# Moving a 64 KB prior ahead of the first load in a mixture-of-softmaxes kernel

## The chip, the cores and the metric

The kernel runs on one core of a Trainium2 chip. The metric is the device time of one execution in microseconds (us); lower is better. A run on one core is compared with runs of the kernel before on the same chip in the same rounds. "MB" is 10^6 bytes.

## The reference

```python
# logits: 32 x 128 x 4 x 4096 float32, prior: 32 x 128 x 4 float32
prior_probs = softmax(prior, axis=-1)            # over the 4 heads
softmax     = softmax(logits, axis=-1)           # over 4096 entries, for each head
mixture     = np.sum(prior_probs[..., None] * softmax, axis=2)   # 32 x 128 x 4096
```

268.4 MB of logits come in, 67.1 MB of result go out, and the prior is 64 KB.

## The kernel before

The rows are worked in 32 units of 128 rows. A unit's load is 8.4 MB (128 partitions of 64 KB), its store 2.1 MB. ScalarE (ACT) takes the exponentials with their sums, VectorE (DVE) the reciprocals and the weighted sum of the four heads, GpSimd (POOL) the small products of coefficients. Loads go out on SP's queue into two buffers, stores on ACT's queue (the last few on SP's). Unit 0 is loaded in two halves, and the first half has already been pulled ahead of the barrier with which the program opens:

```python
def early_first_load(nc):
    blocks = nc.main_func.blocks
    first = next((b, i) for b in blocks[1:] for i in b.instructions
                 if i.engine == mybir.EngineType.SP and i.opcode == "DMACopy")
    block, ins = first
    ...
    block.instructions.remove(ins)
    at = next(...)                     # SP's Drain in the opening block
    blocks[0].instructions.insert(at, ins)
...
        load(0)                                   # SP: two halves, 4.2 MB each
        nc.scalar.dma_start(out=pr, in_=pv)       # ACT: the prior, 16 rows of 4 KB
        load(1)                                   # SP: 8.4 MB
        nc.gpsimd.memset(pn, 0.0)
        nc.vector.reduce_max(pmax, pr, axis=AX.X)
        ...                                       # softmax of the prior, transposes into pp
            if u + 2 < U:
                load(u + 2)                       # waits for unit u's first add
```

The prior's weights `pp` are first read when unit 0's coefficients are formed.

The softmax here doesn't subtract the row's maximum and nothing guards it: scores larger than these inputs give would overflow.

Of the kernel before, what the change touches and what calls it, by code (L numbers as in the profile page):

```python
# [10 lines left out]
AX = mybir.AxisListType  # L11


def early_first_load(nc):





    blocks = nc.main_func.blocks  # L20
    first = next(
        (b, i)
        for b in blocks[1:]
        for i in b.instructions
        if i.engine == mybir.EngineType.SP and i.opcode == "DMACopy"
    )
    block, ins = first
    assert not ins.sync_info.on_wait
    block.instructions.remove(ins)
    at = next(  # L30
        n
        for n, i in enumerate(blocks[0].instructions)
        if i.engine == mybir.EngineType.SP and i.opcode == "Drain"
    )
    blocks[0].instructions.insert(at, ins)


@with_exitstack
def kernel(
    ctx: ExitStack,  # L40
    tc: tile.TileContext,
    logits: bass.AP,
    prior: bass.AP,
    out: bass.AP,
):
    nc = tc.nc
    nc.at_finalize(early_first_load)
    B, S, H, V = logits.shape
    assert prior.shape == (B, S, H)
    assert out.shape == (B, S, V)  # L50
    P = 128
    J = 2
    R = P * J
    G = B * S // R
    U = G * J
    assert G * R == B * S and G <= 32 and H == 4

    lg = logits.rearrange("b s h v -> (b s) h v").rearrange("(g p j) h v -> g j p h v", p=P, j=J)
    ov = out.rearrange("b s v -> (b s) v").rearrange("(g p j) v -> g j p v", p=P, j=J)
    pv = prior.rearrange("b s h -> (b s) h").rearrange("(g r) h -> g r h", r=R)  # L60

    cpool = ctx.enter_context(tc.tile_pool(name="cpool", bufs=1))
    psum = ctx.enter_context(tc.tile_pool(name="psum", bufs=1, space=bass.MemoryType.PSUM))



    before = {}

    def only(ins, *keep):
        for k in keep:  # L70
            tc.add_manual_dep(
                ins.ins,
                k.ins.name,
                mybir.DependencyInfo(mybir.DependencyClass.Sync, mybir.DependencyReason.DATA),
                reason="all that this instruction waits for",
            )
        tc.declare_no_dep(
            ins.ins,
            group="loop",
            keep=[k.ins for k in keep] + before.get(ins.ins.engine, []),  # L80
            reason="covered by the waits that are kept",
        )
        tc.add_to_no_dep_group("loop", ins.ins)
        before[ins.ins.engine] = [ins.ins]
        return ins


    ltile = cpool.tile([P, 2, H, V], FP32, name="ltile")
    loads = {}
    exps = {}  # L90
    adds = {}
    stores = {}

    def load(u):
        if u == 0 or u >= U - 3:
            cuts = (0, 2, 3, 4) if u == U - 1 else (0, 2, 4)
        else:
            cuts = (0, H)
        for h, to in zip(cuts, cuts[1:]):
            ld = nc.sync.dma_start(  # L100
                out=ltile[:, u % 2, h:to], in_=lg[u // J, u % J, :, h:to, :]
            )


            if u >= 2:
                only(ld, adds[u - 2, 0] if h == 0 else exps[u - 2, to - 1])
            else:
                only(ld)
            for k in range(h, to):
                loads[u, k] = ld  # L110

    def store(u, acc, eng, lo=0, hi=V):
        st = eng.dma_start(out=ov[u // J, u % J, :, lo:hi], in_=acc[:, lo:hi])
        stores[u] = only(st, adds[u, H - 1])


    pr = cpool.tile([G, R, H], FP32, name="pr")
    pn = cpool.tile([32, H, R], FP32, name="pn")
    pmax = cpool.tile([G, R], FP32, name="pmax")
    pp = cpool.tile([P, J, H, 32], FP32, name="pp")  # L120


    dsum = cpool.tile([P, U, H], FP32, name="dsum")
    rden = cpool.tile([P, U, H], FP32, name="rden")
    coeff = cpool.tile([P, U, H], FP32, name="coeff")



    ebuf1 = cpool.tile([P, V], FP32, name="ebuf1")
    ebuf2 = psum.tile([P, V], FP32, name="ebuf2")  # L130
    ebuf3 = cpool.tile([P, V], FP32, name="ebuf3")
    obuf = cpool.tile([P, 2, V], FP32, name="obuf")

    with tc.manual_schedule():
        load(0)
        nc.scalar.dma_start(out=pr, in_=pv)
        load(1)
        nc.gpsimd.memset(pn, 0.0)  # L138
        nc.vector.reduce_max(pmax, pr, axis=AX.X)  # L139
        nc.vector.tensor_sub(pr, pr, pmax.unsqueeze(2).to_broadcast([G, R, H]))  # L140
        nc.scalar.activation(pr, pr, AF.Exp)  # L141
        nc.vector.reduce_sum(pmax, pr, axis=AX.X)  # L142
        nc.vector.reciprocal(pmax, pmax)  # L143
        nc.vector.tensor_mul(  # L144
            pn[0:G].rearrange("g h r -> g r h"), pr, pmax.unsqueeze(2).to_broadcast([G, R, H])
        )
        pq = pn.rearrange("g h (p j) -> g j h p", j=J)
        for t in range(P // 32):
            nc.vector.transpose(pp[32 * t : 32 * (t + 1)], pq[:, :, :, 32 * t : 32 * (t + 1)])  # L149

        for u in range(U):
            bufd = u < U - 2
            lt = ltile[:, u % 2]
            acc = obuf[:, u % 2] if bufd else lt[:, 0]
            es = (lt[:, 0], ebuf1, ebuf2, ebuf3) if bufd else [lt[:, h] for h in range(H)]
            ppu = pp[:, u % J, :, u // J]

            def exp(h, *keep):
                ex = nc.scalar.activation(  # L159
                    es[h], lt[:, h], AF.Exp, accum_out=dsum[:, u, h : h + 1]  # L160
                )
                keep = (loads[u, h],) + keep
                if bufd and h and u:
                    keep += (adds[u - 1, h],)
                exps[u, h] = only(ex, *keep)

            def weigh(h, n, *keep):
                rc = nc.vector.reciprocal(rden[:, u, h : h + n], dsum[:, u, h : h + n])  # L168
                only(rc, exps[u, h + n - 1])
                mul = nc.gpsimd.tensor_mul(  # L170
                    coeff[:, u, h : h + n], rden[:, u, h : h + n], ppu[:, h : h + n]
                )
                return only(mul, rc, *keep)

            def add(h, mul, lo=0, hi=V):
                if h == 0:
                    st = nc.vector.tensor_scalar(  # L177
                        out=acc[:, lo:hi], in0=es[h][:, lo:hi], scalar1=coeff[:, u, h : h + 1],
                        scalar2=None, op0=ALU.mult,
                    )  # L180
                    adds[u, h] = only(st, mul)
                else:
                    st = nc.vector.scalar_tensor_tensor(  # L183
                        out=acc[:, lo:hi], in0=es[h][:, lo:hi], scalar=coeff[:, u, h : h + 1],
                        in1=acc[:, lo:hi], op0=ALU.mult, op1=ALU.add,
                    )
                    adds[u, h] = only(st, mul, adds[u, h - 1])

            free = (stores[u - 2],) if bufd and u >= 2 else ()

            m = H if u < U - 4 else 2
            for h in range(H):
                late = h == H - 1 and 4 <= u < U - 3
                if h == H - 1 and 0 < u < U - 3:
                    store(u - 1, obuf[:, (u - 1) % 2], nc.scalar)
                exp(h, *((stores[u - 4],) if late else ()))
                if (h + 1) % m:
                    continue
                g = h + 1 - m
                mul = weigh(g, m, *(free if g == 0 else ()))  # L200
                for k in range(g, h + 1):
                    n = 2 if u == U - 1 and k == H - 1 else 1
                    w = V // n
                    for c in range(n):
                        add(k, mul, c * w, (c + 1) * w)
                        if n > 1:
                            store(u, acc, nc.sync, c * w, (c + 1) * w)
            if u + 2 < U:
                load(u + 2)
            if u == U - 3:  # L210
                store(u - 1, obuf[:, (u - 1) % 2], nc.sync)
                store(u, acc, nc.sync)
            elif u == U - 2:
                store(u, acc, nc.sync)
# [30 lines left out]
```

## Time and profile before

| | before |
|---|---|
| device time, median of 6 runs | 781.04 us (780.79 to 781.23) |
| span from first to last instruction | 779.28 us |
| bytes moved | 335.66 MB, mean 431 GB/s |
| DVE, ACT busy | 67%, 60% |

The span is taken from the first instruction, which is SP's issue of unit 0's first half at 0.00. The time of a profiled run is 1.78 to 1.80 us longer than its span (the one of before took 781.07), in every run but one, which is named below. Two more lines matter later, the DMA queues on the page of before (packets, MB, share of the 16 engines' span; q1 is SP's queue, q10 is ACT's):

```profile
q1 hardware_dynamic: 6048, 276.83, 82.3%
q10 hardware_dynamic: 4064, 58.79, 17.6%
```

Nearly all of q10 is stores; the prior is 0.07 MB of it.

### The profile page before, as it was taken

The page shows a single profiled execution, that of the slowest core. Times are in us where ns is not written, and L with a number is a line of the kernel's source. Part 1 is how long each engine was busy: PE and PEld are TensorE (multiplying, and loading weights), DVE is VectorE, ACT ScalarE, POOL GpSimd, SP SyncE. Part 2 cuts the span into 40 slices and gives each one's busy share as a digit, 9 for nine tenths or more (in the row PEclk, how much of TensorE's full clock was granted, in tenths as well). Part 3 has the DMA queues.
Part 4 walks back from the last instruction along what each step waited for, and adds up shares of the span by engine and source line. Part 5 has one row for each costly group of instructions (what it writes and reads, how often), then busy time and mean ns, then how long its engine had stood idle before and what let it go on. Part 6 is the DMA issues. An engine that isn't in the chain of part 4 may idle for free.

```text
span 779.3 us, 654 instructions
## 1 busy us (share of the span) xinstructions
DVE 521.0 (67%) x174; ACT 466.7 (60%) x258; POOL 8.3 (1%) x41
## 2 busy tenths in 40 slices
DVE  4447875558755587555775557855578655689886
ACT  4476555775457755577555675546765567657782
POOL 0000000000000000000000000000000000000000
DMA  9999999999999999999999999999999999999998
GB/s 407 457 417 401 470 407 434 428 461 428 405 467 403 458 420 433 442 443 418 431 454 407 454 408 467 420 415 447 432 442 417 463 399 463 410 427 433 434 429 377
DMA packets 10117, 335.66 MB, mean 431 GB/s; under 512 B 1136, under 2 KB 1136, under 8 KB 1152
## 3 DMA queue, kind: packets, MB, share of 16 engines
q1 hardware_dynamic: 6048, 276.83, 82.3%
q10 hardware_dynamic: 4064, 58.79, 17.6%
q14 instruction: 5, 0.04, 0.0%
HBM read 268.50 MB, written 67.11 MB: 431 GB/s over the span
## 4 chain that ended last, share of the span: by engine, by line
DMA 64%; ACT 27%; DVE 6%; issue 2%; POOL 0%; DVEq 0%; POOLq 0%
DMA ltile<-in_logits_dram 62%; ACT ebuf L159 19%; ACT ltile L159 8%; DVE obuf L177 5%; DMA out_dram<-obuf 2%; DVE ltile L183 1%; POOL coeff L170 0%; DVE rden L168 0%; DVEq L240 0%; POOLq L240 0%; POOLq L170 0%
## 5 line engine op out<-in xcount | busy, mean ns | idle before, releaser
L183 DVE SCALAR_TENSOR_TENSOR obuf<-ebuf,coeff,obuf 128x4096 f32<-128x4096 f32 x90 | 403.6, 4484 | 3.8 <-POOL coeff L170 0.6
L159 ACT ACTIVATE ebuf<-ltile 128x4096 f32<-128x4096 f32 x90 | 322.9, 3589 | 7.4 <-DMA ltile<-in_logits_dram 7.4
L159 ACT ACTIVATE ltile<-ltile 128x4096 f32<-128x4096 f32 x38 | 137.3, 3614 | 280.6 <-DMA ltile<-in_logits_dram 280.6
L168 DVE RECIPROCAL rden<-dsum 128x4 f32<-128x4 f32 (+1 forms) x36 | 6.3, 175 | 227.9 <-ACT ebuf L159 225.1
L177 DVE TENSOR_SCALAR obuf<-ltile,coeff 128x4096 f32<-128x4096 f32 x30 | 70.6, 2353 | 10.2 <-POOL coeff L170 10.2
L183 DVE SCALAR_TENSOR_TENSOR ltile<-ltile,coeff 128x4096 f32<-128x4096 f32 (+1 forms) x7 | 27.0, 3875 | 0.8 <-POOL coeff L170 0.6
L159 ACT ACTIVATION_READ_ACCUMULATOR ebuf<-ltile 128x1 f32 x90 | 16.8, 186 | 0.0
L170 POOL TENSOR_TENSOR coeff<-rden,pp 128x4 f32<-128x4 f32 (+1 forms) x36 | 7.2, 200 | 755.3 <-DVE rden L168 745.4
L159 ACT ACTIVATION_READ_ACCUMULATOR ltile<-ltile 128x1 f32 x38 | 7.1, 186 | 0.0
L139 DVE TENSOR_REDUCE pmax<-pr 16x256 f32<-16x1024 f32 x1 | 1.2, 1208 | 7.8 <-DMA pr<-in_prior_dram 7.8
L141 ACT ACTIVATE pr<-pr 16x1024 f32<-16x1024 f32 x1 | 1.1, 1055 | 7.8 <-DVE pr L140 7.8
L177 DVE TENSOR_SCALAR ltile<-ltile,coeff 128x4096 f32<-128x4096 f32 x2 | 4.7, 2354 | 0.6 <-POOL coeff L170 0.6
L144 DVE TENSOR_TENSOR pn<-pr,pmax 16x1024 f32<-16x1024 f32 x1 | 1.9, 1939 | 0.1
L141 ACT ACT_TABLE_LOAD x1 | 1.3, 1283 | 1.2 <-PEq L229 1.2
L142 DVE TENSOR_REDUCE pmax<-pr 16x256 f32<-16x1024 f32 x1 | 1.2, 1207 | 1.1 <-ACT pr L141 1.1
L149 DVE STREAM_TRANSPOSE pp<-pn 32x256 f32<-32x256 f32 x4 | 1.7, 435 | 0.1
L143 DVE RECIPROCAL pmax<-pmax 16x256 f32<-16x256 f32 x1 | 1.7, 1741 | 0.0
L140 DVE TENSOR_TENSOR pr<-pr,pmax 16x1024 f32<-16x1024 f32 x1 | 1.2, 1211 | 0.0
L138 POOL MEMSET pn<- 32x1024 f32 x1 | 0.9, 941 | 0.3 <-POOLq L229 0.3
L229 POOL MEMSET const-bfloat16-1.0<- 128x1 bf16 x1 | 0.1, 106 | 0.0
L229 POOL MEMSET const-uint8-127<- 128x1 uint8 x1 | 0.1, 106 | 0.0
L229 POOL MEMSET const-float32-0.0<- 128x1 f32 x1 | 0.1, 103 | 0.2 <-issue 0.2
(1 smaller groups left out, 0.1 us busy)
## 6 DMA issues: line engine op xcount, KB each, us to landing
out_dram<-obuf ACTq DMA_DIRECT2D x28, 2048.0 KB, 29.4
ltile<-in_logits_dram SPq DMA_DIRECT2D x7, 4096.0 KB, 26.1
ltile<-in_logits_dram SPq DMA_DIRECT2D x2, 2048.0 KB, 30.9
out_dram<-obuf SPq DMA_DIRECT2D x2, 2048.0 KB, 33.9
out_dram<-ltile SPq DMA_DIRECT2D x1, 2048.0 KB, 17.2
out_dram<-ltile SPq DMA_DIRECT2D x2, 1024.0 KB, 4.8
ltile<-in_logits_dram SPq DMA_DIRECT2D x28, 30.9
pr<-in_prior_dram ACTq DMA_DIRECT2D x1, 64.0 KB, 7.0
```

Source lines behind the costliest of these rows:

```text
L139: nc.vector.reduce_max(pmax, pr, axis=AX.X)
L140: nc.vector.tensor_sub(pr, pr, pmax.unsqueeze(2).to_broadcast([G, R, H]))
L141: nc.scalar.activation(pr, pr, AF.Exp)
L142: nc.vector.reduce_sum(pmax, pr, axis=AX.X)
L143: nc.vector.reciprocal(pmax, pmax)
L144: nc.vector.tensor_mul(pn[0:G].rearrange("g h r -> g r h"), pr, pmax.unsqueeze(2).to_broadcast([G, R, H]))
L149: nc.vector.transpose(pp[32 * t : 32 * (t + 1)], pq[:, :, :, 32 * t : 32 * (t + 1)])
L159: ex = nc.scalar.activation(es[h], lt[:, h], AF.Exp, accum_out=dsum[:, u, h : h + 1])
L168: rc = nc.vector.reciprocal(rden[:, u, h : h + n], dsum[:, u, h : h + n])
L170: mul = nc.gpsimd.tensor_mul(coeff[:, u, h : h + n], rden[:, u, h : h + n], ppu[:, h : h + n])
L177: st = nc.vector.tensor_scalar(out=acc[:, lo:hi], in0=es[h][:, lo:hi], scalar1=coeff[:, u, h : h + 1], scalar2=None, op0=ALU.mult,)
L183: st = nc.vector.scalar_tensor_tensor(out=acc[:, lo:hi], in0=es[h][:, lo:hi], scalar=coeff[:, u, h : h + 1], in1=acc[:, lo:hi], op0=ALU.mu ...
```

## The change

The intent: have the prior come first, so that its softmax no longer waits behind large load packets, and take the issue off ACT. The prior goes to the head of SP's queue, and both it and the first half of unit 0 are issued ahead of the opening barrier.

```diff
-def early_first_load(nc):
+def early_transfers(nc):
...
+    body = next(b for b in blocks[1:] if of_sp(b, "DMACopy"))
+    for ins in of_sp(body, "DMACopy")[:2]:
+        assert not ins.sync_info.on_wait
+        body.instructions.remove(ins)
+        drain = of_sp(blocks[0], "Drain")[0]
+        blocks[0].instructions.insert(blocks[0].instructions.index(drain), ins)
...
     with tc.manual_schedule():
+        nc.sync.dma_start(out=pr, in_=pv)
         load(0)
-        nc.scalar.dma_start(out=pr, in_=pv)
         load(1)
```

More of the change, by code (lines that the diff above doesn't have):

```diff
@@ L11, with of_sp @@
 AX = mybir.AxisListType
-def early_first_load(nc):
+def early_transfers(nc):
     blocks = nc.main_func.blocks
-    first = next(
-        (b, i)
-        for b in blocks[1:]
-        for i in b.instructions
-        if i.engine == mybir.EngineType.SP and i.opcode == "DMACopy"
-    )
-    block, ins = first
-    assert not ins.sync_info.on_wait
-    block.instructions.remove(ins)
-    at = next(
-        n
-        for n, i in enumerate(blocks[0].instructions)
-        if i.engine == mybir.EngineType.SP and i.opcode == "Drain"
-    )
-    blocks[0].instructions.insert(at, ins)
+    def of_sp(block, opcode):
+        return [
+            i
+            for i in block.instructions
+            if i.engine == mybir.EngineType.SP and i.opcode == opcode
+        ]
+    body = next(b for b in blocks[1:] if of_sp(b, "DMACopy"))
[4 more added lines that the diff above has]
+        blocks[0].instructions.insert(blocks[0].instructions.index(drain), ins)
 @with_exitstack
@@ L46 @@
     nc = tc.nc
-    nc.at_finalize(early_first_load)
+    nc.at_finalize(early_transfers)
     B, S, H, V = logits.shape
```

## The prediction

> **What bounds the kernel now.** I read the page from the top: the busy shares first, then the slices with the DMA row, then the table of stretches, then the chain of waits, and last the opening and the first unit in the timeline.
>
> ```profile
> DVE 521.0 (67%) x174; ACT 466.7 (60%) x258; POOL 8.3 (1%) x41
> DMA  9999999999999999999999999999999999999998
> DMA packets 10117, 335.66 MB, mean 431 GB/s; under 512 B 1136, under 2 KB 1136, under 8 KB 1152
> ```
>
> No compute engine is above 67%, while the DMA engines are at nine tenths or more in 39 of 40 slices. The stretches (length, busy time of DVE, ACT and POOL, clock, DMA share, GB/s) say where the rate is not full:
>
> ```profile
> 0.00:25.00 25.00, 9.04 (x9) 12.26 (x7) 1.15 (x5) 1.00 1.02 422
> 100.00:400.00 300.00, 197.89 (x63) 176.72 (x98) 2.61 (x13) 1.00 1.00 433
> 770.00:779.30 9.30, 3.42 (x2) 0.00 (x0) 0.00 (x0) 1.00 0.76 318
> ```
>
> In the middle the transfers run at 433 GB/s. 335.66 MB at that rate are 775.2 us of the span of 779.3, so only 4.1 us in all are not explained by bytes. The start lacks 25 x (1 - 422/433) = 0.64 us and the last stretch 9.3 x (1 - 318/433) = 2.5 us; the rest is rounding and the middle's small dips. So the start can give back at most about 0.6 us, unless bytes vanish, and the change removes none. The stretch shares are coarse (a short one can show over 1), so I take only sums of long ones.
>
> The chain of waits confirms it (start us, us, what):
>
> ```profile
> 0.79 21.57 DMA ltile<-in_logits_dram
> 22.39 7.32 ACT ebuf L159 x4
> ...
> 30.22 2.37 DVE obuf L177
> 32.60 31.96 DMA ltile<-in_logits_dram
> ```
>
> The prior is not in it. The chain does pass through compute: unit 2's load is only issued at 32.60, after unit 0's first add. But in the timeline unit 1's first exp starts at 41.73, on a load that was issued at 1.18. So at 32.60 the load queue still has some 9 us of unit 1 to move, and the queue doesn't run dry. What sets the end is when the stream of load bytes begins and how fast it runs, and not when an early compute instruction ends.
>
> The opening and the prior's own path, in the timeline (start us, us, engine, line):
>
> ```profile
> 0.00 0.38 SPq L100 DMA_DIRECT2D ltile<-in_logits_dram  x1
> 0.79 0.33 SPq L100 DMA_DIRECT2D ltile<-in_logits_dram  x1
> 0.79 0.39 ACTq L136 DMA_DIRECT2D pr<-in_prior_dram  x1
> 7.81 1.21 DVE L139 TENSOR_REDUCE pmax<-pr 16x256 f32<-16x1024 f32 x1 [7.81 <-DMA pr<-in_prior_dram]
> 16.45 1.78 DVE L149 STREAM_TRANSPOSE pp<-pn 32x256 f32<-32x256 f32 x4
> 29.98 0.20 POOL L170 TENSOR_TENSOR coeff<-rden,pp 128x4 f32<-128x4 f32 x1 [28.26 <-DVE rden L168]
> ```
>
> The first half of unit 0 is already ahead of the opening barrier: issued at 0.00, with the second half and the prior both at 0.79 behind it. The prior's softmax ends at 16.45 + 1.78 = 18.23. The first reader of its result, the coefficient at 29.98, waits for the denominators. The prior has 29.98 - 18.23 = 11.75 us to spare.
>
> **What the Trainium skill says.** "Perfetto Trace Analysis", section Roofline, holds that one core streaming alone is bounded by its 16 DMA engines at about 435 GB/s; the 433 above agree. "DMA: Bandwidth & Descriptors", section Issuing engines are not separate DMA queues, says that transfers started from different engines end up on the same 16 DMA engines and interleave, so that moving an issue saves only sequencer time. The trace agrees: the prior's 64 KB took 7.0 us to land beside the first half of unit 0. The same page, Anatomy of one DMA, gives some 2 us of fixed cost for a transfer (fitted there for the GpSimd path), mostly the receipt after the last byte. Here the first half lands 12.6 us after its issue and the second at 0.79 + 21.57 = 22.36, 9.7 us later, which is just 4.19 MB at 431 GB/s. So the fixed part of a single transfer is 12.63 - 9.73 = 2.9 us, and a transfer behind another in the same queue does not pay it again: it overlaps.
>
> **The change, part by part.**
> The words of the change say that prior and first half are issued early, but the first half was early before. What is new is the prior alone.
> 1. Removed: one issue on ACT's queue (0.39 us at 0.79). ACT next loads its table at 1.21 and then has nothing to do until its exp of the prior at 10.29. Worth 0 at the end.
> 2. Added: one issue on SP, ahead of the first half. In the trace, two issues behind each other on SP start 0.39 us apart (0.79 and 1.18). So the first half is issued at about 0.39 where it was at 0.00. This is on the path: the stream of load bytes starts 0.39 us later. Cost +0.39 us.
> 3. In that gap the prior's own bytes move. 64 KB at 431 GB/s are 0.15 us; before, they took their share out of the same engines a little later. So 0.15 us of the 0.39 are not lost. Credit -0.15 us. Sum of 2 and 3: +0.24 us.
> 4. Moved: SP comes to the opening barrier about 0.39 us later, so the second half goes out at about 1.18 in place of 0.79, unit 1 at about 1.57 in place of 1.18, and POOL's memset and ACT's table load also slide by 0.4. The first half keeps the queue full until about 10 us, so none of these is waited for. Cost 0.
> 5. Gained off the path: the prior no longer shares the engines with the first half's large packets. An estimate from the fixed 2.9 us above is a landing about 2 to 3 us after issue, against 0.79 + 7.0 = 7.8. DVE's five operations on the prior and its four transposes start about 5 us earlier and end at about 13.3 in place of 18.23. Slack grows from 11.75 to about 17 us. Worth 0. ACT does its exp of the prior at about 5.4 instead of 10.29, in time where it was idle either way.
>
> So unit 0 lands at about 12.9 and 22.6, every later load slides by the same 0.24, the span is 779.5 and the time 781.04 + 0.24 = 781.3 us.
>
> **The rivals.**
> - The start is pre-paid. If the first transfer of a queue pays a start-up of its own that the prior now pays, the first half follows at once and begins no later, and what the prior saves by not sharing may even show. For it: 2.9 us of fixed cost, of which I can't see how much comes before the first byte, and a start that lacks 0.64 us of bytes. Against: SP must still spend 0.39 us on the first issue before it can make the second. It would make 780.8 to 781.0.
> - The prior's landing matters. If the early compute were on the path, 5 us less would show and the time would be about 776. Against it: 11.75 us of slack, and ACT's first exp of logits at 12.66 is released by its own load, not by the prior. I give it almost nothing.
> - The prior's fixed cost is paid in series. If the first half could not stream until the prior's receipt was in, the whole stream would start 2 to 2.9 us later: 783 to 784. Against it: the two halves land 9.7 us apart, with no gap between transfers of one queue. A few per cent.
> - The interleaving of loads and stores takes another phase. The chain goes through a store near the end (18.06 us, from 700.23, before a coefficient at 718.42), and the first periods of two units differ from the later ones (start of the load piece at 32.60, 82.00 and 129.75; later every 48.35). A shift of 0.24 us could be swallowed or doubled there. This is worth some 0.3 us either way and is most of my range.
>
> **Range and chances.** The three times of before lie within 0.19 us, so the noise is small against the terms. The centre is 781.3. Downwards the pre-paid start reaches 780.8. Upwards the full 0.39 without credit gives 781.4, and a phase shift on top of it some 781.9. A serial fixed cost lies outside. 2% are 15.6 us; nothing above comes near that, as even the whole start, with the prior on the path, is 5 us. I give 0.01 to faster, 0.98 to within 2% and 0.01 to slower.
>
> **What would show each step right or wrong.** In the timeline of the changed kernel: the prior's issue at 0.00 on SP's queue and the first half's at about 0.39 (step 2), the second half's at about 1.2 (step 4), DVE's first reduction at about 3 and not 7.81 (step 5). The first exp of logits should start at about 12.9 and the exp behind the second half at about 22.6 (sum of 2 and 3): at 12.66 and 22.39 or earlier the start was pre-paid; at 15 the fixed cost was in series. The load pieces of the chain after 300 us should stand 0.2 to 0.3 later than before, with the same 48.35 us between them. If the opening shows +0.24 and the end another amount, the phase of the stores took or added the rest. The prediction is wrong as a whole if the middle rate departs from 433 GB/s, since 1% of it is 7.8 us.

## The result, and the profile after

| | before | after |
|---|---|---|
| median of 6 runs | 781.04 us (780.79 to 781.23) | 781.41 us (781.36 to 782.33) |
| span of the profiled run | 779.28 us | 779.58 us |

The ratio is 1.0007, with a 95% interval of 0.9995 to 1.002: the same within 2%, and the interval includes 1. A ratio here is the mean time of one kernel's fast runs over that of the other's in the same rounds, so one long run (782.33) weighs on it and not on the medians. In rank the difference is clear: all six runs of after are longer than all six of before. By medians it is +0.37 us.

The page of after names the same bytes and the same busy shares. Its queue lines show the move: 32 packets (16 of data and 16 that tell of the landing) have gone from q10 to q1.

```profile
q1 hardware_dynamic: 6080, 276.89, 82.3%
q10 hardware_dynamic: 4032, 58.72, 17.6%
```

The opening in the timeline of after (start us, us, engine, line, what, idle time before):

```profile
0.00 0.39 SPq L134 DMA_DIRECT2D pr<-in_prior_dram  x1
0.45 0.42 SPq L99 DMA_DIRECT2D ltile<-in_logits_dram  x1
1.28 0.33 SPq L99 DMA_DIRECT2D ltile<-in_logits_dram  x1
2.26 1.21 DVE L138 TENSOR_REDUCE pmax<-pr 16x256 f32<-16x1024 f32 x1 [2.26 <-DMA pr<-in_prior_dram]
10.86 1.78 DVE L148 STREAM_TRANSPOSE pp<-pn 32x256 f32<-32x256 f32 x4
29.96 0.20 POOL L169 TENSOR_TENSOR coeff<-rden,pp 128x4 f32<-128x4 f32 x1 [27.75 <-DVE rden L167]
```

The prior lands 2.2 us after its issue where it took 7.0, and its weights are ready at 12.64 and not at 18.23. The coefficient that reads them still starts at 29.96 (29.98 before). The first half of unit 0 is issued 0.45 us later. Now the first exp of units 0, 1 and 2, in the timeline of before:

```profile
12.66 3.62 ACT L159 ACTIVATE ltile<-ltile 128x4096 f32<-128x4096 f32 x1 [1.31 <-DMA ltile<-in_logits_dram]
41.73 3.62 ACT L159 ACTIVATE ltile<-ltile 128x4096 f32<-128x4096 f32 x1 [12.04 <-DMA ltile<-in_logits_dram]
64.58 3.62 ACT L159 ACTIVATE ltile<-ltile 128x4096 f32<-128x4096 f32 x1 [8.35 <-DMA ltile<-in_logits_dram]
```

And in that of after:

```profile
12.64 3.62 ACT L158 ACTIVATE ltile<-ltile 128x4096 f32<-128x4096 f32 x1 [6.83 <-DMA ltile<-in_logits_dram]
41.70 3.62 ACT L158 ACTIVATE ltile<-ltile 128x4096 f32<-128x4096 f32 x1 [12.03 <-DMA ltile<-in_logits_dram]
64.97 3.62 ACT L158 ACTIVATE ltile<-ltile 128x4096 f32<-128x4096 f32 x1 [8.77 <-DMA ltile<-in_logits_dram]
```

This was the surprise. Units 0 and 1 land when they did before, in spite of the later issue; the difference appears between 42 and 65 us, while unit 2's load and the first store are under way. After that it stays. Load pieces of the chain of waits, before and then after:

```profile
82.00 30.32 DMA ltile<-in_logits_dram
...
323.93 30.91 DMA ltile<-in_logits_dram
...
662.50 30.89 DMA ltile<-in_logits_dram
```

```profile
82.39 30.32 DMA ltile<-in_logits_dram
...
324.25 30.91 DMA ltile<-in_logits_dram
...
662.80 30.89 DMA ltile<-in_logits_dram
```

**A closer look at the packets.** The trace holds a record of each DMA packet: queue, start, duration and bytes, though not which of the 16 engines moved it. Packets follow each other without a gap, and most of one size take the same time: 0.61 us for the 16 KB of a store packet, 1.21 for 32 KB of a half, 2.42 for 64 KB of a unit (medians). A few take longer. I call the excess the stretch of a packet; summed over packets and divided by 16 engines it is a time of the whole stream. (Each engine's first large packet is stretched in every kernel, 0.5 to 0.7 us in this sense; the columns below leave that out.) Sewing packets together where one starts as another ends gives what one engine does. This is worked out from the records and is not a view of the profile (an engine's chain can be swapped for that of another in step with it). The columns are start in us, queue, size, duration in us, and the stretch at the places that matter:

```
before                          after
 1.05 q1   32 KB  1.89           1.05 q1    4 KB  0.30   the prior
 2.94 q1   32 KB  1.21           1.65 q1   32 KB  1.93   first half begins
 4.14 q1   32 KB  1.21           3.58 q1   32 KB  1.21
 5.35 q10   4 KB  0.16 prior     4.78 q1   32 KB  1.21
 5.51 q1   32 KB  1.55 +0.34     5.99 q1   32 KB  1.21
 7.06 q1   32 KB  1.21           7.20 q1   32 KB  1.21
...
48.22 q1   64 KB  2.45          48.30 q1   64 KB  2.79   +0.37
50.66 q10  16 KB  0.61          51.08 q10  16 KB  0.61   first store begins
51.27 q1   64 KB  2.42          51.69 q1   64 KB  2.46
...
60.33 q1   64 KB  2.88 +0.46    60.84 q1   64 KB  2.91   +0.49   unit 2's last packet
63.21 q10  16 KB  0.61          63.75 q10  16 KB  0.61
```

Two things are read from it. First, before, the prior costs the load stream 0.16 us of its own and a stretch of 0.34 in the packet behind it. Second, after, that stretch is gone, and one of about the same size stands where the first store comes in. From 50.7 us on, load and store packets alternate with no stretch until unit 2's last packet. "DMA: Bandwidth & Descriptors", section Queues, rings and completion order, of the Trainium skill says that each engine goes round its queues packet by packet; the alternation of one q1 and one q10 packet agrees. It doesn't tell of a stretch.

The **lag** sums this up: at a time t, it is t less the transfer work done by then, where work is the usual duration of each packet, summed and divided by 16 engines. With equal bytes, the lag that is left in the steady state is what a kernel loses.

| lag in us, at | 5 us | 45 us | 66 us | 100 us | stretch 5 to 45 | stretch 45 to 66 |
|---|---|---|---|---|---|---|
| before | 1.76 | 2.12 | 2.63 | 2.56 | 0.42 | 0.56 |
| after | 2.15 | 2.09 | 3.00 | 2.93 | 0.00 | 0.96 |

At 100 us the lags differ by 2.93 - 2.56 = 0.37 us. That this is just the difference of the medians is in part luck: the spans of these two traces differ by 0.30, and the second trace of before (below) has a lag of 2.38. Read one trace to about 0.2 us. The start is 2.15 - 1.76 = 0.39 later; the prior's missing stretch gives that back by 45 us; and between 45 and 66 us it is lost again. So is the cost the start, or is it the first store? The experiments are about that.

### The profile page after: what moved, and what is told of

Its sections match the earlier page's. It is cut to its first block, busy times and chain, and to the rows that moved or that the text cites. A ratio compares the mean times of both kernels' runs of the same rounds, so it can differ in the third digit from the quotient of the medians.

```text
span 779.6 us, 654 instructions
## 1 busy us (share of the span) xinstructions
DVE 521.0 (67%) x174; ACT 466.7 (60%) x258; POOL 8.3 (1%) x41
## 4 chain that ended last, share of the span: by engine, by line
DMA 64%; ACT 27%; DVE 6%; issue 2%; POOL 0%; DVEq 0%; POOLq 0%
DMA ltile<-in_logits_dram 62%; ACT ebuf L158 19%; ACT ltile L158 8%; DVE obuf L176 5%; DMA out_dram<-obuf 2%; DVE ltile L182 1%; POOL coeff L169 0%; DVE rden L167 0%; DVEq L239 0%; POOLq L239 0%; POOLq L169 0%
```

## The experiments

The theories, as the expectations name them: I is my recorded sum (later issue, less the prior's bytes). F: the first transfer on ACT's queue costs 0.35 us, and after the change that is a store. P and V: the stretch at the first store depends on chance or phase. Later ones are said where they were formed. Where a result names a profiled run's time, that is one run. No interval of a ratio below clearly excludes 1, as 0.3 us is 0.04% of the time; I use the separation of the runs instead.

### The changed kernel again

> The changed kernel itself again, as the base for the others on this chip. All theories: 781.4 us, 0.3 to 0.5 above the kernel before on the same chip; in its timeline unit 0's first exp at 12.64, unit 1's at 41.70, unit 2's at 64.97.

Measured: 781.45 us (781.25 to 782.68, 5 runs) against 781.02 (780.83 to 781.19, 9 runs of before). The exps start at 12.70, 41.77 and 65.05, the stretch from 45 to 66 us is 0.91. Result and place repeat.

### The kernel before again

> The kernel before itself, for a second trace of it. Theory R (the two stretches of load packets, 0.08 us per DMA engine at the first store near 48 us and 0.47 at the end of unit 2's load near 60, belong to the kernel and repeat): same two numbers within 0.05, unit 2's exp at 64.6. Theory V (they vary from run to run, so the 0.3 that the changed kernel loses there is chance): other numbers, anywhere from 0.1 to 0.4 and 0 to 0.5. Time 781.0 either way.

Measured: 780.83 us (780.80 to 781.05) against 780.94. Its two stretches are not those of the first trace: about 0.4 at the first store and 0.03 at the end of unit 2's load, where it was 0.09 and 0.47. But their sum from 45 to 66 us is 0.44 (0.56 in the first), and unit 2's exp starts at 64.31. So R is wrong for each stretch alone, and V's "anywhere" is wrong for the sum: the sum sets before (0.44, 0.56) apart from after (0.91, 0.96).

### e1: the order of the two early transfers swapped

```diff
-        nc.sync.dma_start(out=pr, in_=pv)
         load(0)
...  (inside load, behind the first half of unit 0)
+            if u == 0 and h == 0:
+                nc.sync.dma_start(out=pr, in_=pv)
```

> Both transfers still ahead of the barrier on SP's queue, but the first half of unit 0 first and the prior second. Theory F (the first transfer on ACT's queue costs some 0.35 us per DMA engine wherever it falls: in the kernel before it was the prior, in the changed one it is the first store): the stream starts 0.45 us sooner than in the changed kernel, nothing is switched to and fro at 5 us, first exp at about 12.15, unit 1's at about 41.4, but the first store still pays, so unit 2's exp is 0.7 us less ahead than in the changed kernel's gap: near 64.6; time 781.1. Theory I (my recorded sum: the later issue costs 0.39, the prior's bytes give back 0.15, and nothing else): 781.15. Theory P (the first store's extra time depends on where between two load packets it comes, not on first use): start as under F, then anything from 780.8 to 781.1.

Measured: 780.97 us (780.77 to 781.28) against 781.02. The order alone takes back what the change lost. But the path is not as F had it: the first exp starts at 16.44, as ACT's exp of the prior stands ahead of it and the prior now lands behind the half, at 12.96. Unit 0's first add slides to 31.45, and still unit 1's exp starts at 41.80. This is a clean sign that early compute has room: ACT was 3.8 us late there, and the time didn't move. The packet behind the prior is stretched here too (0.39 between 5 and 45 us), though there is only one queue then. The stretch from 45 to 66 us is 0.43, with ACT's queue never used before the first store, where F has 0.35 more than in before (0.44 to 0.56): F is against the evidence. The second half and unit 1 are issued here at 1.25 and 1.64, as late as in the change (1.28 and 1.66), so it is not their delay that costs.

### e2: ACT's queue used once at the start

```diff
+        nc.scalar.dma_start(out=warm, in_=pv[:, 0, 0:1])   # 16 x 4 bytes, issued ahead of the barrier
```

> The changed kernel plus one transfer of 16 x 4 bytes on ACT's queue, ahead of the barrier, into a tile that nobody reads; SP's two early issues as they are. Theory F: the first use of ACT's queue is paid at the start where the engines idle, the first load packets beside the first store no longer stretch, unit 2's exp at about 64.6 instead of 64.97, time 781.1. Theories I and P: an extra transfer can't help, unit 2's exp stays at 64.97 and the time at 781.4.

Measured: 781.23 us (781.07 to 781.89) against 781.02. The first store's packets stretch as without it (0.40 from 45 to 55 us, 1.00 from 45 to 66). F falls: the queue had been used. The median is between the theories, and the profiled run is one of the long ones (781.83): in it 15 of the 16 engines finish unit 2's load by 64.85 and one at 66.14. The other side is open too: three of the five runs are at 781.07 to 781.23, only 0.05 to 0.21 above before, though the first half is issued as late as in the change. None of them was profiled, so what gave part of the delay back isn't known. Whether such a straggler (an engine that ends late) also makes the changed kernel's long runs (782.33, 782.21 and 782.68 in 11) is open; none of them was the profiled one.

### e3: both early, each on its own queue

```diff
-        nc.sync.dma_start(out=pr, in_=pv)
         load(0)
+        nc.scalar.dma_start(out=pr, in_=pv)      # ACT's first transfer, moved ahead of the barrier too
```

> The first half of unit 0 first and alone early on SP's queue, as before; the prior on ACT's queue, as before, but issued ahead of the barrier too. Theory F: neither the issue delay nor the stretched packet at 5 us nor the first store's stretch is paid, so unit 0's first exp at about 12.3, unit 1's at about 41.4, unit 2's at about 64.2, time 780.7, 0.3 below the kernel before and 0.7 below the changed one. Theory I: as the kernel before, 781.0. Theory P: the start gains 0.34, the first store takes back 0 to 0.3: 780.7 to 781.0. DVE's first reduction at about 2.5 to 3 in any case.

Measured: 780.89 us (780.75 to 781.30) against 781.02, interval 0.9988 to 1.0013. The largest distance below before (the second set of before had 780.83 in other rounds), but 0.13 us with overlapping runs is no gain. The first half is at 0.00 again; the prior lands at 5.50; its stretch is there (the lag goes from 1.80 at 3 us to 2.14 at 5), the first exp is at 12.81 and not at 12.3. From 45 to 66 us the stretch is only 0.26.

### e4: the first store on SP's queue

```diff
-                    store(u - 1, obuf[:, (u - 1) % 2], nc.scalar)
+                    store(u - 1, obuf[:, (u - 1) % 2], nc.sync if u == 1 else nc.scalar)
```

> The changed kernel with the first store alone moved from ACT's queue to SP's, where it stands behind unit 2's load; the second store is then the first on ACT's queue. Theory Q (the stretch at 48 us comes of two queues starting to share the engines): no stretch near 48 us, unit 2's load lands some 3 us sooner as no store packets lie between, and the 0.37 us shows near 75 us instead, at the second store; time as the changed kernel, 781.4. Theory O (it is tied to this moment, an ACT-queue store beside a full load queue early on): it is gone and does not come back; time 780.7 to 781.1.

Measured: 782.33 us (782.17 to 782.52) against 780.94, the interval of the ratio 1.0000 to 1.0033. Both theories miss. Nothing stretches at 48 us and unit 2 lands 2.7 us sooner (62.24 in place of 64.95), but its last load packets, which have the store behind them in the same queue, take 3.6 in place of 2.42 us, a stretch of 1.2, and another 0.50 follows from 75 to 85 us where the second store begins. The interruption isn't tied to a second queue, and it is dearer here: 1.39 us above before of the same rounds, where the change is 0.37 to 0.43 above its own.

### e5: no transfer of the prior at all (a wrong result)

```diff
-        nc.scalar.dma_start(out=pr, in_=pv)
         load(1)
         nc.gpsimd.memset(pn, 0.0)
+        nc.vector.memset(pr, 0.0)
```

> The kernel before without the transfer of the prior (its tile is filled with zeros on chip, so the result is wrong on purpose). Theory N (the prior costs some 0.35 us of transfer time beyond its 0.15 us of bytes, wherever it stands): unit 0's first exp at 12.66 - 0.5 = 12.15, the second half's at 21.9, unit 1's at 41.2; time 780.5 if the later stretches are those of the kernel before. Theory B (it costs its bytes only): 12.5 and 780.9. Theory F, already against the evidence, would have the first store pay 0.35 here, as ACT's queue is used for the first time: 780.85.

Measured: 781.12 us (781.03 to 781.15) against 780.94. This was the run that turned the theory. The first exps of units 0, 1 and 2 in its timeline:

```profile
11.89 3.62 ACT L159 ACTIVATE ltile<-ltile 128x4096 f32<-128x4096 f32 x1 [6.35 <-DMA ltile<-in_logits_dram]
40.95 3.62 ACT L159 ACTIVATE ltile<-ltile 128x4096 f32<-128x4096 f32 x1 [12.04 <-DMA ltile<-in_logits_dram]
64.32 3.62 ACT L159 ACTIVATE ltile<-ltile 128x4096 f32<-128x4096 f32 x1 [8.86 <-DMA ltile<-in_logits_dram]
```

Units 0 and 1 are 0.77 and 0.78 us ahead of before, even more than N expected, and at unit 2 the lead is 0.26 (against 64.58) or nothing (against 64.31 of the second trace). The stretch from 45 to 66 us is 0.97. So the 0.35 us that the prior costs the stream at 5 us is not saved by having no prior: the first store takes it. The span is 779.11, between those of the two traces of before (779.28 and 779.04). The time is longer all the same, since in this profiled run alone 2.03 us of it lie outside the span; I can't say why.

### e6: the prior loaded twice ahead of the first half

```diff
         nc.sync.dma_start(out=pr, in_=pv)
+        nc.sync.dma_start(out=pr2, in_=pv)
...
-    for ins in of_sp(body, "DMACopy")[:2]:
+    for ins in of_sp(body, "DMACopy")[:3]:
```

> The changed kernel with the prior loaded twice ahead of the first half on SP's queue, all three early (the second copy into a tile that nobody reads): the suspected issue cost doubled. Recorded step 2 (each issue ahead of the first half delays the stream by 0.4 us, bytes hidden in the gap): first half issued at 0.88, its first packets at about 1.95 instead of 1.5, unit 0's first exp at about 13.1, time 781.85. If the start were pre-paid (first rival of the prediction), unit 0's exp would stay at 12.64 to 12.8 and the time at 781.4 to 781.55.

Measured: 781.65 us (781.63 to 781.67) against 780.94. The half is issued at 0.89 and its first packets start at 1.94, as expected; the first exp starts at 12.98, and the time is 0.71 above before of its rounds, where the change with one copy is 0.37 and 0.43 above: 0.28 to 0.34 for the second copy (0.24 by the bare medians, 781.65 and 781.41). The direction of step 2 is right and the pre-paid start is not, but the forecast of +0.44 left out the credit of step 3: the first large packets start 0.38 us later than in the change (2.08 against 1.70, means of the first 16), and the second copy's 0.15 us of bytes move in that gap, which would leave 0.23. The measured 0.28 to 0.34 lies between 0.23 and 0.38 and doesn't show the credit.

Here a pattern shows. Where the prior's packets come among the loads (before, e1, e3) little is stretched from 45 to 66 us: 0.26 to 0.56. Where nothing comes among them before the first store (after, e2, e5, e6) it is 0.81 to 1.00. So I formed theory H: a running load stream loses a certain amount when it is first interrupted, by whatever.

### e7: the change, with a second copy of the prior on ACT's queue

```diff
         load(0)
+        nc.scalar.dma_start(out=pr2, in_=pv)
         load(1)
```

> The changed kernel plus a second copy of the prior on ACT's queue behind the barrier, where the kernel before has the only one (into a tile that nobody reads). Theory H (a running load stream loses some 0.35 to 0.45 us the first time that other packets come between its own, and once only: in the kernel before the prior pays it at 5 us, in the changed one the first store at 48): the stretched packet of +0.35 is back at about 5 to 6 us, unit 0's exp at 12.64 + 0.5 = 13.15, and the two stretches at 48 and 60 us fall from 0.92 in sum to about 0.5, so the time is only the extra bytes, 0.15, above the changed kernel: 781.55. Theory A (each interruption pays for itself and they add): stretches at 48 and 60 stay at 0.9, time 781.9.

Measured: 781.49 us (781.37 to 781.51) against 781.06. The stretch at 5 us is back (0.43 between 5 and 45 us), the first exp starts at 13.30, and the stretch from 45 to 66 us falls from 0.96 to 0.36. The time is 0.43 above before, that of the change (0.37, 0.43) plus at most the copy's bytes. A would have 781.9.

### e8: the kernel before, with a second copy on ACT's queue

```diff
         nc.scalar.dma_start(out=pr, in_=pv)
+        nc.scalar.dma_start(out=pr2, in_=pv)
```

> The kernel before plus a second copy of the prior right behind the first on ACT's queue. Theory H: the first prior packet pays the 0.35, the second none or little, only its bytes: unit 0's exp at 12.66 + 0.15 to 0.2 = 12.85, the sum of the stretches at 48 and 60 us stays near 0.45, time 781.15. Theory A: a second stretch of 0.35 beside the second copy, exp at 13.15, time 781.5.

Measured: 781.23 us (781.04 to 781.51) against 781.06. The time is H's, the way is not: the second copy does stretch its neighbour, 1.01 us in all between 5 and 45, and then the store finds nothing left to take (0.01 from 45 to 66). In the timeline:

```profile
13.48 3.62 ACT L161 ACTIVATE ltile<-ltile 128x4096 f32<-128x4096 f32 x1 [2.07 <-DMA ltile<-in_logits_dram]
42.54 3.62 ACT L161 ACTIVATE ltile<-ltile 128x4096 f32<-128x4096 f32 x1 [12.04 <-DMA ltile<-in_logits_dram]
64.96 3.62 ACT L161 ACTIVATE ltile<-ltile 128x4096 f32<-128x4096 f32 x1 [7.92 <-DMA ltile<-in_logits_dram]
```

Against before (12.66, 41.73, 64.58) it is 0.8 us late at units 0 and 1, and 0.4 at unit 2. "Once only" is wrong. What fits is an amount for all interruptions together.

### e9: the issue delay alone

```diff
+        nc.sync.dma_start(out=tiny, in_=pv[:, 0, 0:1])     # 16 x 4 bytes ahead of the first half
         load(0)
         nc.scalar.dma_start(out=pr, in_=pv)                # the prior as in the kernel before
```

> The kernel before with one transfer of 16 x 4 bytes put ahead of the first half on SP's queue, the prior left on ACT's queue behind the barrier: the issue delay of the change alone, without moving the prior. Recorded step 2, as the runs correct it (the stream starts 0.4 to 0.5 us later and nothing gives it back): first half issued at 0.45, first packets at about 1.5, the +0.35 at 5 us as before, unit 0's exp at 13.1, stretches at 48 and 60 us 0.45 in sum as before, time 781.45 to 781.5. If a later start were absorbed at 48 and 60 us (what the run without the prior seems to say): 781.0 to 781.2.

Measured: 781.41 us (781.34 to 781.48) against 781.06 (780.82 to 781.18). The prior stays where it was, only one issue of 64 bytes stands ahead of the first half, and the loss is 0.35 us: that of the whole change (0.37), with no overlap of the runs. In its timeline:

```profile
0.00 0.39 SPq L135 DMA_DIRECT2D tiny<-in_prior_dram  x1
0.45 0.42 SPq L99 DMA_DIRECT2D ltile<-in_logits_dram  x1
13.19 3.62 ACT L160 ACTIVATE ltile<-ltile 128x4096 f32<-128x4096 f32 x1 [1.32 <-DMA ltile<-in_logits_dram]
64.89 3.62 ACT L160 ACTIVATE ltile<-ltile 128x4096 f32<-128x4096 f32 x1 [8.12 <-DMA ltile<-in_logits_dram]
```

The load pieces of its chain at 324.21 and 662.86 stand 0.28 and 0.36 after those of before. The stretches are 0.43 and 0.37, near those of before (0.37 to 0.42 and 0.44 to 0.56). So an issue on SP ahead of the first half is enough for the loss, and with e1, where the prior is also early but behind the half and nothing is lost, it is the cause. The sizes are known less well: the first packets start 0.58 us later than in before (1.74 against 1.16, means of the first 16), with no bytes of the prior in the gap, and only 0.35 of that is lost.

### e10: four interruptions

```diff
         nc.scalar.dma_start(out=pr, in_=pv)
+        for k in range(3):
+            nc.scalar.dma_start(out=spare[:, k], in_=pv[:, 64 * k : 64 * (k + 1)])
```

> The kernel before plus three more small transfers (16 rows of 1 KB, 0.04 us of bytes each) right behind the prior on ACT's queue, into a tile that nobody reads: four interruptions of the first loads instead of one. Theory L (corrected by the run with two: up to the end of unit 2's load the stream loses about 0.9 us in all to being interrupted, however that is spread; whatever the first transfers take is not taken again at 48 and 60 us): stretches between 5 and 20 us of 0.9 to 1.1 in sum, none left at 48 and 60, time at most 0.12 of bytes plus 0.2 above the kernel before, 781.2 to 781.3. Theory A (every interruption costs its own 0.35 to 0.45 and they add): stretches of 1.6 in sum by 20 us and 0.45 more at 48 and 60, time 782.2.

Measured: 781.55 us (781.31 to 781.75, 5 runs) against 780.99 (780.86 to 781.32, 9 runs). The stretches are 1.19 between 5 and 45 us and 0.01 from 45 to 66. Theory L is right that nothing is left for the store and that the amounts don't add up (A: 782.2), and its limit of 0.9 to 1.1 is too low for four interruptions: the time is 0.25 above its range.

### The runs side by side

Lag and stretch in us, from the packet records of each profiled run; the time is the median, with that of before in the same rounds in brackets.

| kernel | first half issued | lag at 5 | stretch 5 to 45 | stretch 45 to 66 | lag at 100 | time |
|---|---|---|---|---|---|---|
| before | 0.00 | 1.76 | 0.42 | 0.56 | 2.56 | 781.04 |
| before again | 0.00 | 1.73 | 0.37 | 0.44 | 2.38 | 780.83 (780.94) |
| e1 swapped | 0.00 | 1.82 | 0.39 | 0.43 | 2.47 | 780.97 (781.02) |
| e3 both early, two queues | 0.00 | 1.80 (at 3 us) | 0.09 (and 0.34 before 5) | 0.26 | 2.32 | 780.89 (781.02) |
| e5 no prior | 0.00 | 1.69 | 0.01 | 0.97 | 2.48 | 781.12 (780.94) |
| e8 two on ACT | 0.00 | 1.81 | 1.01 | 0.01 | 2.65 | 781.23 (781.06) |
| e10 four on ACT | 0.00 | 1.83 | 1.19 | 0.01 | 2.86 | 781.55 (780.99) |
| after | 0.45 | 2.15 | 0.00 | 0.96 | 2.93 | 781.41 (781.04) |
| after again | 0.44 | 2.22 | 0.00 | 0.91 | 2.95 | 781.45 (781.02) |
| e2 ACT used early | 0.45 | 2.17 | 0.00 | 1.00 | 2.99 | 781.23 (781.02) |
| e7 change, one more on ACT | 0.44 | 2.11 | 0.43 | 0.36 | 2.73 | 781.49 (781.06) |
| e9 tiny transfer ahead | 0.45 | 2.25 | 0.43 | 0.37 | 2.89 | 781.41 (781.06) |
| e6 two ahead | 0.89 | 2.32 | 0.14 | 0.81 | 3.09 | 781.65 (780.94) |
| e4 first store on SP | 0.45 | 2.16 | 0.00 | 1.20 (and 0.50 after) | 3.69 | 782.33 (780.94) |

The kernels that issue the first half at 0.00 reach 100 us with a lag of 2.3 to 2.6 (2.65 and 2.86 with the added transfers of e8 and e10), those that issue it later with 2.7 to 3.1 (e4 aside). The stretches of the two columns add to 0.7 to 1.2 in all but e4 (e3's 0.34 before 5 us counted in), however the small transfers are placed. **What that amount is, is not shown.** A head start of the reads that is used up by the first interruptions would look like this, but no record shows it. Also open is what shares it out between the first store and the end of unit 2's load.

## Why the prediction was right or wrong

The time was right: 781.3 was forecast in a range of 780.8 to 781.9, and 781.41 came; +0.24 forecast by the sum, +0.37 measured. The steps fared differently.

- **What bounds the kernel**: right. The stream of load bytes sets the end, and of early things only its start or more interruptions move it (e10 +0.56, e4 +1.39). e1 delays ACT's first exp by 3.8 us and e5 has unit 0 land 0.77 us sooner, and neither moves the time by more than 0.2. One reading under it was wrong: the first 25 us lack more than 0.64 us. The view counts a packet's bytes whole where it starts; with each packet's bytes shared over its duration I get 396 GB/s there and 25 x (1 - 396/433) = 2.1 us missing, near the lag of 1.76 at 5 us plus the prior's stretch. The ceiling of "about 0.6 us" was therefore too low; the sum didn't use it.
- **Step 1**, ACT's issue is worth nothing: no run takes it alone. The lines after it fit: ACT's table load starts at 1.27 (1.21 before) and ACT still waits for its load.
- **Step 2**, +0.39 for the issue ahead of the first half: right, and shown by e9 alone, +0.35. The half was issued at 0.45 rather than 0.39, and its first packets start at 1.50 where before they start at 1.02 (first of the 32 KB records; the means of the first 16 are 1.70 and 1.16).
- **Step 3**, a credit of 0.15 for the prior's bytes: mis-sized for the opening, and not shown for the end. Behind those bytes the kernel before also loses 0.34 us in the next packet, so at units 0 and 1 the change had made good the whole delay (12.64 against 12.66), where I wanted 12.9. What it had made good was then lost beside the first store. By the packets the delay of the start (1.70 - 1.16 = 0.54), less the 0.15, is 0.39, the difference of the lags at 5 us, and 0.37 was measured. But e9, which has no such credit, lost 0.35 and not 0.15 more than the change. The two traces of before differ by 0.18 in lag at 100 us, as much as the credit, so these runs can't show it.
- **Step 4**: right. The second half is issued at 1.28 and unit 1 at 1.66, and nothing waits for them (in e1 they are as late and nothing is lost).
- **Step 5**: right. The prior lands at 2.2 us, the transposes end at 12.64 (13.3 forecast), and none of it shows at the end.
- **The sum**, +0.24, was 0.13 short of the medians' difference. Which term was mis-sized is open: by the packets it is step 2 (0.39 by the spacing of issues, 0.54 by the start of the packets), by e9 against the change it is the credit of step 3. That 0.24 came as near is in part luck, as the sum knew nothing of the stretches.
- **The rivals.** By my own test ("at 12.66 and 22.39 or earlier the start was pre-paid") the first rival would have won: 12.64 and 22.36. The test was wrong, not only the forecast of 12.9. A landing at 12 us doesn't tell whether the start was free when another saving of the same size stands between; e6 and e9 tell. The phase of loads and stores, the last rival, did move things by 0.4 us, but as a loss that is taken at one place or another. Chance remains in it: the two traces of before differ by 0.17 in the sum of their stretches. The prediction's last test fits: the opening showed -0.02 and the end +0.3 to +0.4, and what lay between was at the first store. The prior's landing and a serial fixed cost are out: 5 us less wait moved nothing, and the prior's landing at 2.2 us didn't hold back packets that started at 1.50.
- **The chain**: load pieces after 300 us stand 0.32 (324.25 against 323.93) and 0.30 (662.80 against 662.50) later with the same period, at the upper edge of the forecast 0.2 to 0.3.

No version of these beats both kernels by more than the runs scatter.

## What to carry to other kernels

In a kernel that its transfers bound, put nothing ahead of the first large load on the queue that issues it: even 64 bytes cost 0.35 us of the end here (e9), while a small transfer that is needed only later cost nothing that the runs show behind it (e1) or on another queue (e3). A saving that shows at the first landings isn't yet a saving at the end: follow it past the first point where loads and stores meet, and compare work done, not landing times. And when a small cost is to be taken away, ask what would take its place: here the run without the prior at all was no faster.

## What the Trainium skill lacked or had wrong

- "DMA: Bandwidth & Descriptors", section Issuing engines are not separate DMA queues, calls the time to initiate a transfer usually small relative to the DMA itself. That holds (0.33 to 0.44 us against 12.6), but it doesn't say that an issue ahead of the first transfer delays everything behind it: +0.35 us at the end for 64 bytes (e9), with issues 0.42 to 0.45 us apart at the opening (e1, after, e6).
- The same page, section Queues, rings and completion order, has packets of queues take turns, and the trace agrees; it lacks that the first such turns stretch a neighbouring load packet: 1.55 in place of 1.21 us behind a 4 KB packet, up to 0.6 us at the first store (e5), 0.7 to 1.2 us in all by 66 us (e4 aside, and each engine's first large packet left out), and only 0.19 in the whole rest of the kernel before.
